# S5's Toeplitz rows and outputs: four groups one after the other in one row of PSUM, or side by side in four column tiles of TensorE

## The chip, the core and the metric

The kernel runs on one core of a Trainium2 chip. The core has TensorE (PE: matmuls, with weight loads shown apart as PEld), VectorE (DVE), ScalarE (ACT), GpSimd (POOL) and SyncE (SP), which issues most DMAs. Each engine works through its own queue in order and waits on semaphores for the others. The metric is the device time of one execution in microseconds.

## What is computed

One block of a model with two streams of 256 tokens and width 2048: modulation from two conditioning vectors, a projection `w_in`, three mixers beside each other (S5, a gated delta net, an mLSTM), a projection `w_out`, and a gated FFN. Everything is fp32. The change lies in S5, which has 32 groups of 16 channels and 64 complex states in each of two directions:

```python
def s5_run(inputs, state0, par):
    (u,) = inputs
    ab_re, ab_im, bb_re, bb_im, c_re, c_im = par
    bu_re = jnp.einsum('gph,btgh->btgp', bb_re, u)
    bu_im = jnp.einsum('gph,btgh->btgp', bb_im, u)
    ...
    ar, ai, sr, si = lax.associative_scan(complex_affine_combine, (a_re, a_im, bu_re, bu_im), axis=1)
    ...
    y = jnp.einsum('ghp,btgp->btgh', c_re, s_re) - jnp.einsum('ghp,btgp->btgh', c_im, s_im)
    return y, (s_re[:, -1], s_im[:, -1])
```

The two directions are added, `d * u` is added, and the sum goes through gelu and a gated linear unit.

## The kernel before

The kernel writes its work as generators that run beside each other. `feed` is the stream of the large matmuls (tiles `wf`, split into `wh` and `wl`, multiplied into banks `s`); each `yield` of S5 pulls so many microseconds of that stream between S5's own steps. `side` is a second stream, the modulation vectors: tiles `vw` are loaded (three buffers) and accumulated into `vacc` on VectorE, one step for one load. The program is then put in an order for each engine by a scheduler, so that rows of the order differ from the order of the text; within an engine the order is fixed when the kernel runs.

S5 works on chunks of 8 tokens. Matmuls give each chunk's contribution to the state (`s_part`), a scan on VectorE runs over the chunks (`scan`), and its states are laid out as `Sc` by two copies on VectorE and two on ScalarE. The output of a chunk is then its start state times a table `cf`, plus the chunk's own inputs `U` times a Toeplitz matrix `toe`. The 32 groups go in 8 batches of NB = 4:

- `cf_tables` builds the two parts (real and imaginary) of a batch's table, all on GpSimd: for each part 8 products of 128x128 and one sum of 128x512. Each part has two buffers, so the table of batch b+2 can begin only when `y_part(b)` has read that of batch b.
- `k_part` makes the Toeplitz rows. Matmuls `k<-cf,bz` give for each group 32 rows (16 for each direction) of 128 columns; a copy on ScalarE brings them to SBUF as `k2`; `dd`, the middle block with `d` on its diagonal, is added on VectorE. The rows are written to the scratch `kscr` in DRAM by DMAs on SP, and read back, shifted for each of 8 tokens, by four DMAs on ScalarE's queue into `toe`. (The profile calls both the matmul's bank and `k2` "k", also the bank of `dd`'s small matmuls `k<-c_re,bbre` and `k<-ncim,bbim`.)
- `y_part` makes the outputs: three matmuls for each group, `Sc` part 0, `Sc` part 1, `toe`, accumulated in the bank `y`; a copy to `yb`; after every second batch eight transposes `yT` and a copy to `yf`.

`k_part` of batches 0 and 1 runs beside the scan; then `y_part(b)` and `k_part(b+2)` alternate. After batch 7 come the gelu, the gated unit (`glu`, `sg`, `mx`), and the next stage, `gates`.

Before the change the four groups of a batch stand one after the other in the free dimension of one bank, in its partitions 0 to 31: `o_ = pk[0:32, g * P:(g + 1) * P]`, likewise for `py`. One copy of 32x512 takes a bank out. All lines are those of the functions printed here; the profile names helpers, so matmuls are L107, transposes L111, SP's DMAs L135, ScalarE's DMAs L138, products and sums L156, vacc steps L159 and L163, and ScalarE's copies L167.

Of the kernel before, what the change touches and what calls it, by code (L numbers as in the profile page):

```python
# [80 lines left out]
def body(tc, ins, out):  # L81
# [34 lines left out]
    with es:  # L116
# [885 lines left out]
        if 0 == 0:  # L1002
            z_units(m1, "stg")

        kscr = drp.tile([16, 32, 272], F32, name="kscr")
        NB = 4

        def s5(s1, s2):
# [64 lines left out]
            for g0 in range(0, 32, NB):  # L1073
                ens = []
                for part in range(2):
                    en_ = s2.tile([P, NB, 8, 16], F32, tag=f"en{part}", name="en")
                    if part == 0:
                        table(en_, pe[:, :, 0], bbre, pe[:, :, 1], bbim, g0, ALU.subtract, DVE, "ttmp")
                    else:
                        e_, t_ = (DVE, "ttmp") if g0 // NB in () else (POOL, "ttmq")  # L1080
                        table(en_, pe[:, :, 0], bbim, pe[:, :, 1], bbre, g0, ALU.add, e_, t_)
                    ens.append(en_)
                yield (1.3 if g0 else 1.3) * 1.3
                if pend is not None:
                    yield from s_part(pend, *pens)
                else:
                    bz = s1.tile([P, 2, 32, 32], F32, name="bz")
                    DVE.memset(bz, 0.0)
                    for i, b_ in enumerate((bbre, bbim)):
                        for d in range(2):  # L1090
                            r = slice(64 * d, 64 * d + 64)
                            copy(bz[r, i, :, 16 * d:16 * d + 16], b_[r].rearrange("p h g -> p g h"))
                pend, pens = g0, ens
            yield 1.3 * 1.3
            yield from s_part(pend, *pens)
# [56 lines left out]
            def k_part(b_):  # L1152
# [11 lines left out]
                   dT[:, gs].unsqueeze(2).to_broadcast([16, NB, 16]), ALU.mult)  # L1164
                yield 5.0 * 1.1
                pk = bank("k")
                for g in range(NB):
                    o_ = pk[0:32, g * P:(g + 1) * P]
                    PE.matmul(o_, bz[:, 0, g0 + g], cf[0][:, g], start=True, stop=False)
                    PE.matmul(o_, bz[:, 1, g0 + g], cf[1][:, g], start=False, stop=True)  # L1170
                k2 = s2.tile([32, NB, P], F32, tag="en0", name="k2")
                tt(dd, dd, pk0[0:16, 0:NB * 16].rearrange("p (g h) -> p g h", h=16), ALU.add)
                copy(k2.rearrange("p g c -> p (g c)"), pk[0:32])
                dma(kscr[:, gs, 0:P], k2[16:32])
                dma(kscr[:, gs, 144:272], k2[0:16])
                dma(kscr[:, gs, P:144], dd)
                toe = s2.tile([P, NB, P], F32, tag="eT", name="toe", bufs=3)
                yield 0.6 * 1.1
                for g in range(NB):
                    a = kscr[:, g0 + g, 16:144]  # L1180
                    (dma, dma_a, dma_p)[(1, 1, 1, 1)[g]](toe[:, g], bass.AP(a.tensor, a.offset, [[16, 8], list(a.ap[0]), list(a.ap[1])]))
                toes[b_] = toe

            def y_part(b_):
# [1 line left out]
                cf, toe = cfs.pop(b_), toes.pop(b_)  # L1186
                Sc = scs[0]
                py = bank("y")
                for g in range(NB):
                    o_ = py[0:32, g * P:(g + 1) * P]  # L1190
                    PE.matmul(o_, Sc[:, 0, g0 + g], cf[0][:, g], start=True, stop=False)
                    PE.matmul(o_, Sc[:, 1, g0 + g], cf[1][:, g], start=False, stop=False)
                    PE.matmul(o_, U[:, g0 + g, 32:64], toe[:, g], start=False, stop=True)
                if b_ % 2 == 0:
                    yT[0] = s1.tile([32, 8, 2 * NB, 16], F32, tag="Sctx", name="yb")
                yb = yT[0]
                copy(yb[:, :, NB * (b_ % 2):NB * (b_ % 2) + NB], py[0:32].rearrange("c (g j h) -> c j g h", j=8, h=16))
                if b_ % 2:
                    ps = bank("yT")
                    for j in range(8):  # L1200
# [926 lines left out]
```

## Time and profile before

| | us |
|---|---|
| median of 3 runs (lowest, highest) | 1821.02 (1817.79, 1821.43) |
| the profiled execution | 1827.01 |
| its span, first to last instruction | 1825.2 |
| PE busy | 1649.1 (90%) |
| DVE busy | 1111.4 (61%) |
| ACT busy | 762.3 (42%) |
| POOL busy | 443.6 (24%) |

The shares are means over stages with different limits. S5 begins at about 165 us, its scan runs from about 254 to 313, `y_part` and `k_part` alternate from 313 to 424, and the gated unit ends at about 457. A granted clock of 1.00 in a stretch is TensorE's 2.4 GHz level, 0.50 its 1.2 GHz level. An fp32 matmul of this kind is two records in the trace, so 8 records are four matmuls.

### The profile page before, as it was taken

The numbers are of one execution on the slowest core, as the hardware profiler recorded it, in microseconds if no ns is written. First come the engines' busy times: TensorE is split into PE (matmuls) and PEld (weight loads), VectorE is DVE, ScalarE is ACT, GpSimd is POOL, SyncE is SP. The second block draws the span as 40 slices with busy tenths as digits, with TensorE's granted clock in tenths as the row PEclk, the third lists the DMA queues.
The fourth block names the chain that finished last, engine by engine and source line by source line (L and its number), as shares of the span: only waits on it lengthen the run. The fifth ranks groups of instructions, "written<-read, shape, count | busy, mean of one in ns | idle before, by whom it ended". The sixth has DMA issues, their size and how long they took to land. (4 is left out here: it accounts for less than half of the span.)

```text
span 1825.2 us, 25461 instructions
## 1 busy us (share of the span) xinstructions
PE 1649.1 (90%) x9476; PEld 1336.5 (73%) x9476; DVE 1111.4 (61%) x1724; ACT 762.3 (42%) x1277; POOL 443.6 (24%) x409
## 2 busy tenths in 40 slices
PE   3986798889789998997899959999999999999998
PEld 1645687777578777776677748888888888888886
DVE  4417958666766778778544488667565454444444
ACT  3314222223354425357456475444444444443443
POOL 1014862991131343136454320000000000000001
PEclk9988998999879998999999979999999999999999
DMA  9987222667565656553222439778776666655553
GB/s 330 336 297 174 60 84 77 188 190 234 172 192 178 196 167 214 156 156 111 94 70 82 173 127 315 246 238 278 205 243 193 187 192 188 207 196 195 191 192 136
DMA packets 209202, 340.42 MB, mean 187 GB/s; under 512 B 24517, under 2 KB 68123, under 8 KB 208183
## 3 DMA queue, kind: packets, MB, share of 16 engines
q1 hardware_dynamic: 202215, 330.06, 57.3%
q0 software_dynamic: 1936, 5.60, 1.1%
q10 hardware_dynamic: 4928, 3.15, 0.6%
q8 instruction: 74, 1.21, 0.3%
q14 instruction: 49, 0.40, 0.1%
HBM read 332.11 MB, written 6.64 MB: 186 GB/s over the span
## 5 line engine op out<-in xcount | busy, mean ns | idle before, releaser
L167 ACT ACTIVATE wh<-wf 128x1024 fp32r<-128x1024 f32 (+1 forms) x404 | 420.8, 1044 | 566.5 <-PE s L107 457.7
L156 DVE TENSOR_TENSOR wl<-wf,wh 128x1024 fp32r<-128x1024 f32 (+1 forms) x350 | 430.0, 1232 | 362.9 <-ACT wh L167 359.7
L107 PE MATMUL s<-wl,h2h 128*128 128x512 f32 x704 | 276.4, 393 | 7.3 <-DVE wl L156 7.3
L107 PE MATMUL s<-wh,h2h 128*128 128x512 f32 x704 | 276.5, 394 | 6.8 <-ACT wh L167 4.1
L107 PE MATMUL s<-wh,h2l 128*128 128x512 f32 x704 | 276.3, 392 | 1.7 <-DVE h2l L156 1.7
L159 DVE SCALAR_TENSOR_TENSOR vacc<-vw,cT,vacc 128x512 f32<-128x512 f32 x240 | 204.4, 852 | 78.5 <-DMA vw<-in_ada_w_dram 75.4
L156 POOL TENSOR_TENSOR wl<-wf,wh 128x1024 fp32r<-128x1024 f32 x54 | 134.7, 2495 | 268.1 <-ACT wh L167 226.0
L156 POOL TENSOR_TENSOR rs<-ss,mhalf 128x1 f32<-128x1 f32 x6 | 4.8, 798 | 747.4 <-ACT ps L167 747.4
L107 PE MATMUL s<-hh,wh 128*128 128x512 f32 (+1 forms) x448 | 170.9, 394 | 3.3 <-ACT hh L167 3.3
L107 PE MATMUL s<-hh,wl 128*128 128x512 f32 (+1 forms) x448 | 164.1, 372 | 6.5 <-DVE wl L156 4.8
L107 PE MATMUL s<-hl,wh 128*128 128x512 f32 (+1 forms) x448 | 166.3, 372 | 0.0
L107 PEld LDWEIGHTS s<-wl,h2h 128*128 128x128 f32 x704 | 133.4, 189 | 35.7 <-DVE wl L156 8.1
L107 PEld LDWEIGHTS s<-wh,h2h 128*128 128x128 f32 x704 | 133.3, 189 | 35.5 <-ACT wh L167 5.2
L107 PEld LDWEIGHTS s<-wh,h2l 128*128 128x128 f32 x704 | 133.4, 190 | 29.8 <-DVE h2l L156 2.1
L107 PE MATMUL s<-wh,ah 128*128 128x512 f32 x352 | 136.8, 390 | 0.0
L107 PE MATMUL s<-wh,al 128*128 128x512 f32 x352 | 136.6, 389 | 0.0
L107 PE MATMUL s<-wl,ah 128*128 128x512 f32 x352 | 136.6, 389 | 0.0
L107 PEld LDWEIGHTS s<-hh,wh 128*128 128x128 f32 x448 | 89.0, 200 | 22.0 <-ACT hh L167 7.0
L107 PEld LDWEIGHTS s<-hh,wl 128*128 128x128 f32 x448 | 87.6, 197 | 22.2 <-DVE wl L156 6.1
L107 PE MATMUL s<-wh,mix 128*128 128x512 f32 x256 | 102.6, 428 | 0.1
L107 PEld LDWEIGHTS s<-hl,wh 128*128 128x128 f32 x448 | 88.8, 198 | 15.8 <-issue 3.6
L107 PE MATMUL s<-wl,hh 128*128 128x256 f32 (+1 forms) x256 | 89.6, 352 | 9.8 <-DVE wl L156 9.3
(576 smaller groups left out, 2806.6 us busy)
## 6 DMA issues: line engine op xcount, KB each, us to landing
vw<-in_ada_w_dram SPq DMA_DIRECT2D x256, 256.0 KB
wf<-in_ffn_w_gate_dram SPq DMA_DIRECT2D x96, 512.0 KB
wf<-in_w_in_dram SPq DMA_DIRECT2D x92, 512.0 KB
wf<-in_ffn_w_up_dram SPq DMA_DIRECT2D x88, 512.0 KB
wf<-in_ffn_w_down_dram SPq DMA_DIRECT2D x88, 512.0 KB
wf<-in_ada_w_dram SPq DMA_DIRECT2D x32, 1024.0 KB
wf<-in_w_out_dram SPq DMA_DIRECT2D x32, 512.0 KB
x<-in_x_dram SPq DMA_DIRECT2D x4, 1024.0 KB
```

Of the source, the lines that this page charges most:

```text
L107: return cls.queue(nc.tensor.matmul(*a, **k))
L156: return (eng or DVE).tensor_tensor(out=o, in0=a, in1=b, op=op)
L159: return (eng or DVE).scalar_tensor_tensor(out=o, in0=a, scalar=s, in1=b, op0=op0, op1=op1)
L167: return ACT.activation(out=o, in_=a, func=f, **kw)
```

## The change

For `k` and `y` the matmul of group g writes partitions 32g to 32g+31 of the bank, columns 0 to 127, and the loops run over the parts outside and over the groups inside. The `k` bank is copied out as one 128x128; `bz` holds the two directions' columns the other way round, so that one DMA for each group writes both halves of its rows; `kscr` has the group as its first dimension. The `y` bank is copied out in four pieces of 32x128, on VectorE and ScalarE in turn.

```diff
-        kscr = drp.tile([16, 32, 272], F32, name="kscr")
+        kscr = drp.tile([32, 16, 272], F32, name="kscr")
...
-                            copy(bz[r, i, :, 16 * d:16 * d + 16], b_[r].rearrange("p h g -> p g h"))
+                            copy(bz[r, i, :, 16 - 16 * d:32 - 16 * d], b_[r].rearrange("p h g -> p g h"))
...
                 pk = bank("k")
+                for i in range(2):
+                    for g in range(NB):
+                        PE.matmul(pk[32 * g:32 * g + 32, 0:P], bz[:, i, g0 + g], cf[i][:, g], start=(i == 0), stop=(i == 1))
+                k2 = s2.tile([P, P], F32, tag="en0", name="k2")
+                tt(dd, dd, pk0[0:16, 0:NB * 16].rearrange("p (g h) -> p g h", h=16), ALU.add)
+                copy(k2, pk[:, 0:P])
                 for g in range(NB):
-                    o_ = pk[0:32, g * P:(g + 1) * P]
-                    PE.matmul(o_, bz[:, 0, g0 + g], cf[0][:, g], start=True, stop=False)
-                    PE.matmul(o_, bz[:, 1, g0 + g], cf[1][:, g], start=False, stop=True)
-                k2 = s2.tile([32, NB, P], F32, tag="en0", name="k2")
-                tt(dd, dd, pk0[0:16, 0:NB * 16].rearrange("p (g h) -> p g h", h=16), ALU.add)
-                copy(k2.rearrange("p g c -> p (g c)"), pk[0:32])
-                dma(kscr[:, gs, 0:P], k2[16:32])
-                dma(kscr[:, gs, 144:272], k2[0:16])
-                dma(kscr[:, gs, P:144], dd)
+                    a = kscr[g0 + g, :, 0:P]
+                    dma(bass.AP(a.tensor, a.offset, [[144, 2]] + [list(v) for v in a.ap]), k2[32 * g:32 * g + 32])
+                dma(kscr[gs, :, P:144].rearrange("g h x -> h g x"), dd)
...
-                    a = kscr[:, g0 + g, 16:144]
+                    a = kscr[g0 + g, :, 16:144]
...
                 py = bank("y")
-                for g in range(NB):
-                    o_ = py[0:32, g * P:(g + 1) * P]
-                    PE.matmul(o_, Sc[:, 0, g0 + g], cf[0][:, g], start=True, stop=False)
-                    PE.matmul(o_, Sc[:, 1, g0 + g], cf[1][:, g], start=False, stop=False)
-                    PE.matmul(o_, U[:, g0 + g, 32:64], toe[:, g], start=False, stop=True)
+                for i in range(3):
+                    for g in range(NB):
+                        w, m = (U[:, g0 + g, 32:64], toe[:, g]) if i == 2 else (Sc[:, i, g0 + g], cf[i][:, g])
+                        PE.matmul(py[32 * g:32 * g + 32, 0:P], w, m, start=(i == 0), stop=(i == 2))
...
-                copy(yb[:, :, NB * (b_ % 2):NB * (b_ % 2) + NB], py[0:32].rearrange("c (g j h) -> c j g h", j=8, h=16))
+                for g in range(NB):
+                    (DVE.tensor_copy, copy)[g % 2](yb[:, :, NB * (b_ % 2) + g],
+                                                   py[32 * g:32 * g + 32, 0:P].rearrange("c (j h) -> c j h", h=16))
```

The scheduler's order changes with it. On TensorE, at `y_part(0)` right after the scan, before (here `cf_1825` and `cf_1836` are parts 0 and 1 of batch 0's table, `y_2541` the bank):

```order
L107 MATMUL y_2541<-cf_1825,Sc_2535 32x128 [waits DVE_49,Activation_49]
L107 MATMUL k0_2578<-c_re_335,bbre_391 16x16
L107 MATMUL k0_2578<-ncim_400,bbim_392 16x16
L107 MATMUL k0_2578<-c_re_335,bbre_391 16x16
L107 MATMUL y_2541<-cf_1836,Sc_2535 32x128 [waits DVE_49,Activation_49]
L107 MATMUL y_2541<-toe_1915,U_1128 32x128 [waits DMAHW2_49]
L107 MATMUL y_2541<-cf_1825,Sc_2535 32x128
L107 MATMUL y_2541<-cf_1836,Sc_2535 32x128
L107 MATMUL y_2541<-toe_1915,U_1128 32x128 [waits DMAHW4_49]
```

and after, from the same place to the second k pack of batch 2 (`k_2684`; `y_2712` is `y_part(1)`):

```order
L107 MATMUL y_2545<-cf_1825,Sc_2539 32x128 [waits DVE_49,Activation_49]
L107 MATMUL y_2545<-cf_1825,Sc_2539 32x128 x3
...
L107 MATMUL y_2545<-cf_1836,Sc_2539 32x128 [waits DVE_49,Activation_49]
L107 MATMUL y_2545<-cf_1836,Sc_2539 32x128 x3
L107 MATMUL y_2545<-toe_1917,U_1128 32x128 [waits DMAHW2_49]
...
L107 MATMUL k_2684<-cf_2563,bz_1208 32x128 [waits Pool_49]
L107 MATMUL k_2684<-cf_2563,bz_1208 32x128 x3
L107 MATMUL y_2712<-cf_1943,Sc_2539 32x128 [waits DVE_49]
...
L111 MATMUL yT_2729<-ident_112,yb_2558 128x32 [waits PE_49,Activation_49]
...
L107 MATMUL k_2684<-cf_2574,bz_1208 32x128 [waits Pool_49]
```

All reads of part 0 now stand ahead of the first read of part 1, and the transposes yT, which wait for the copies of batches 0 and 1, stand ahead of the second k pack. Before, 18 matmuls of s stood between `vm` and batch 2's first k; now the 51 that come next stand behind the second pack.

On VectorE, at the same place, before:

```order
L1147 COPY Sc<-Sq 64x1024 [waits DVE_49]
L1147 COPY Sc<-Sq 64x1024
L156 TENSOR_TENSOR wl<-wf,wh 128x1024 [waits DMAHW2_49,Activation_49]
L156 TENSOR_TENSOR dd<-dd,k_2578 16x64 [waits PE_49]
L156 TENSOR_TENSOR mod_1099<-vm,cols 128x4 [waits PE_49]
L163 TENSOR_SCALAR vacc<-vw,cT 128x512 [waits DMAHW4_49]
L156 TENSOR_TENSOR dd<-ident,dT 16x64 [waits DMAHW5_49,DVE_49]
L159 SCALAR_TENSOR_TENSOR vacc<-vw,cT,vacc 128x512 [waits DVE_49] x2
```

and after, where the copies of batch 0 stand at the head and those of batch 1 behind six vacc steps:

```order
L1197 COPY yb<-y 32x8x16 [waits DVE_49,PE_49,Activation_49]
L156 TENSOR_TENSOR dd<-dd,k_2585 16x64 [waits PE_49]
L1197 COPY yb<-y 32x8x16 [waits Activation_49]
L156 TENSOR_TENSOR mod_1099<-vm,cols 128x4 [waits PE_49]
L163 TENSOR_SCALAR vacc<-vw,cT 128x512 [waits DMAHW4_49]
...
L1197 COPY yb<-y 32x8x16 [waits PE_49]
L159 SCALAR_TENSOR_TENSOR vacc<-vw,cT,vacc 128x512 [waits DMAHW6_49,DVE_49]
L1197 COPY yb<-y 32x8x16 [waits Activation_49]
```

In the middle of the vacc steps VectorE now waits for TensorE's y and for ScalarE's copy of the group before; ScalarE's own yb copies wait for VectorE in turn.

On SP, at batch 7's writes, before:

```order
L135 DMA kscr<-k_3522 16x4x128 [waits DMAHW3_49,Activation_49]
L135 DMA kscr<-k_3522 16x4x128
L135 DMA vw<-in_ada_w_dram 128x512 [waits DMAHW7_49,DVE_49]
L135 DMA vw<-in_ada_w_dram 128x512 [waits DMAHW6_49,DMAHW0_49,DVE_49]
L135 DMA wf<-in_w_in_dram 128x2x512 [waits DMAHW3_49,DVE_49]
```

and after:

```order
L135 DMA kscr<-k_3554 2x16x128 [waits Activation_49]
L135 DMA kscr<-k_3554 2x16x128
L135 DMA vw<-in_ada_w_dram 128x512 [waits DMAHW6_49,DMAHW0_49,DVE_49]
L135 DMA kscr<-k_3554 2x16x128
L135 DMA vw<-in_ada_w_dram 128x512 [waits DMAHW2_49,DVE_49]
L135 DMA vw<-in_ada_w_dram 128x512 [waits DMAHW4_49,DMAHW3_49,DVE_49]
L135 DMA kscr<-k_3554 2x16x128 [waits DMAHW5_49]
```

The four writes of a batch are divided by vw loads that wait for VectorE.

## Rows read from the trace of the kernel before

**Rows 1.** Busy us (instructions) by stretch: PE, PEld, DVE, ACT, POOL; clock, DMA share, GB/s

```profile
305.20:313.00 7.80, 0.24 (x3) 0.04 (x1) 7.25 (x32) 1.96 (x2) 0.00 (x0) 0.80 0.00 0
313.00:319.00 6.00, 4.94 (x28) 4.05 (x29) 1.23 (x2) 2.88 (x2) 0.00 (x0) 0.50 0.11 25
319.00:408.40 89.40, 77.29 (x615) 66.30 (x613) 56.50 (x72) 19.52 (x37) 84.64 (x108) 0.96 0.64 186
408.40:424.00 15.60, 14.30 (x85) 11.82 (x86) 6.14 (x9) 3.28 (x5) 0.00 (x1) 0.89 0.62 195
...
440.00:455.00 15.00, 11.67 (x55) 9.04 (x56) 8.70 (x13) 4.98 (x7) 3.20 (x2) 1.00 0.96 305
455.00:520.00 65.00, 46.81 (x229) 37.62 (x228) 46.68 (x71) 26.89 (x44) 14.07 (x11) 0.85 0.65 205
...
1150.00:1800.00 650.00, 650.00 (x2926) 539.37 (x2925) 347.25 (x336) 273.94 (x287) 0.00 (x0) 1.00 0.67 210
```

**Rows 2.** GpSimd in time order: start, us, line, operation, count [idle before <-releaser]

```profile
319.01 4.43 POOL L156 TENSOR_TENSOR cf<-pf,c_re 128x128 f32<-128x128 f32 x8 [18.87 <-PE y L107]
...
335.35 4.23 POOL L156 TENSOR_TENSOR ttmp<-pf,c_im 128x128 f32<-128x128 f32 x4
...
341.00 1.80 POOL L156 TENSOR_TENSOR ttmp<-pf,c_im 128x128 f32<-128x128 f32 x4
...
366.01 5.10 POOL L156 TENSOR_TENSOR cf<-pf,c_re 128x128 f32<-128x128 f32 x8 [3.57 <-PE y L107]
...
406.81 1.59 POOL L156 TENSOR_TENSOR cf<-cf,ttmp 128x512 f32<-128x512 f32 x1
```

**Rows 3.** TensorE's matmuls in time order, two records for one matmul

```profile
313.03 0.64 PE L107 MATMUL y<-cf,Sc 128*32 128x128 f32 x2 [7.59 <-DVE Sc L1147]
...
314.88 0.63 PE L107 MATMUL y<-cf,Sc 128*32 128x128 f32 x2 [1.03 <-ACT Sc L167]
...
318.29 1.06 PE L107 MATMUL y<-cf,Sc 128*32 128x128 f32 x4
...
365.55 0.60 PE L107 MATMUL y<-cf,Sc 128*32 128x128 f32 x4
...
378.01 1.72 PE L107 MATMUL k<-cf,bz 128*32 128x128 f32 x14 [0.42 <-POOL cf L156]
```

**Rows 4.** The ada matmuls in four column tiles, and their weight loads (PEld)

```profile
21.29 1.93 PE L107 MATMUL ada<-wf,csz 128*32 128x512 f32 x8 [0.78 <-DMA wf<-in_ada_w_dram]
...
51.20 1.07 PE L107 MATMUL ada<-wf,csz 128*32 128x512 f32 x8
52.20 2.00 PE L111 MATMUL xt<-ident,x 128*128 128x128 f32 x16
...
51.20 0.16 PEld L107 LDWEIGHTS ada<-wf,csz 128*32 128x32 f32 x8 [0.17 <-issue]
```

**Rows 5.** Small copies out of PSUM, grouped by line: count, busy us, mean ns

```profile
L167 ACT ACTIVATE vn<-st 128x128 f32<-128x128 f32 x24 | 6.5, 272 | 2.2 <-PE st L107 2.0
...
L1309 DVE COPY bec<-beT 128x48 f32<-128x48 f32 x1 | 0.2, 202 | 0.0
```

**Rows 6.** ScalarE and its DMA queue (ACTq) in time order, batch 7

```profile
412.73 0.59 ACT L167 ACTIVATE k<-k 32x512 f32<-32x512 f32 x1 [5.52 <-PE k L107]
...
419.02 2.45 ACTq L138 DMA_DIRECT2D toe<-kscr  x4
...
423.90 0.59 ACT L167 ACTIVATE yb<-y 32x512 f32<-32x512 f32 x1 [0.32 <-PE y L107]
```

**Rows 7.** SP's DMA issues in time order, batch 7's two writes

```profile
414.91 0.85 SPq L135 DMA_DIRECT2D kscr<-k  x2
```

**Rows 8.** VectorE's vacc steps in time order, first and last of nine

```profile
321.25 0.76 DVE L163 TENSOR_SCALAR vacc<-vw,cT 128x512 f32<-128x512 f32 x1
...
328.41 3.48 DVE L159 SCALAR_TENSOR_TENSOR vacc<-vw,cT,vacc 128x512 f32<-128x512 f32 x3 [0.53 <-DMA vw<-in_ada_w_dram]
```

**Rows 9.** Who waited for whom, 424 to 600 us: total, times, longest

```profile
ACT wh L167 <- DMA wf<-in_w_in_dram: 22.0, 7, 6.7
```

## Prediction

> **What bounds the kernel now.** I read the stretches first. From 1150 to 1800 us TensorE is busy in every microsecond [rows 1], so nothing there can hide a late start: whatever S5 gains or loses is likely to reach the end. The change lies in S5, whose last part runs from 313 to about 455 us. In its largest piece, 319.0 to 408.4, GpSimd is busy 84.64 of 89.40 us, TensorE 77.29, VectorE 56.50 and ScalarE 19.52 [rows 1]: GpSimd, which builds the cf tables (16 small products and two sums of 128x512 for a batch), is what fills the time. Its own rows say when it starts and stops [rows 2]. It starts at 319.01 after 18.87 us of waiting for "PE y", that is, until y_part(0) has read the cf tables of batch 0 and their two buffers are free; it waits once more, 3.57 us, again for "PE y", before 366.01; the last sum starts at 406.81. Then TensorE's rows [rows 3]: y_part(0) begins at 313.03, when Sc is there, and its last group at 318.29.
>
> So the question is not how much TensorE time the packing saves, but how much earlier cf is free and how soon the results leave after the last table.
>
> **The change part by part, by TensorE time.** A 128-column fp32 matmul is two records. Unpacked and at the high clock, 14 records took 1.72 us [rows 3], 0.12 each, so four groups (8 records) are 0.98 us. What four column tiles cost shows in the ada matmuls at the head of the kernel, which are laid out this way, in fp32, with 512 columns: 8 records, the next work 1.00 us later, and their eight weight loads within 0.16 us [rows 4]. A quarter of the columns gives 0.25 us as an estimate. Bounds for a pack: 0.25 and 0.98 us; I take 0.25, since the ada rows are the same form. There are 8 x 2 packs of k and 8 x 3 of y, so 40 x 0.73 = 29 us less TensorE work, 0 at the other bound. Of this nearly all turns into waiting for GpSimd, since GpSimd has 4.76 us of slack in the 89.40 and TensorE 12.11.
>
> A page speaks against the packing. The Trainium skill, "TensorE: Matmul & The Clock Gate", Part 3 on row/col tiling, says that weight loads overlap running matmuls only where the row groups differ; column tiles share them, and a pack would then pay its loads, too. With the row's 0.16 us a pack would be 0.41 instead of 0.25, some 6 us over 40 packs, off the path; no row here separates the two, and if the loads weigh more than that, it is the third rival.
>
> **The start of GpSimd's chain.** Before, y goes group by group, and cf part 0 is read last by group 3, at 318.29; GpSimd starts 0.72 later [rows 2, 3]. After, the four matmuls on cf part 0 stand first (the first pair of order listings). They start at 313.03 as before, waiting for Sc. The clock is at its low level there: granted 0.50 from 313 to 319, after 7.8 us in which TensorE was busy 0.24 [rows 1]; a pack of 512 columns at that level took 1.93 us [rows 4], a quarter is 0.48. With 0.3 us to the release (0.72 less the 0.42 of two records, from 0.64 and 1.06 for two and four [rows 3]) GpSimd starts at 313.8: 5.2 us earlier. Part 1 is free at about 315.7, as its matmul waits for ScalarE's Sc until 314.88 [rows 3]; GpSimd is then at the end of its first four products (a free one 0.45, from 1.80 for four [rows 2]). Without overlap of the packs it would be 4 x 0.42 = 1.7, so 315.0: 4.0 us earlier.
>
> **The second wait.** The 3.57 us before 366.01 stand behind group 3 of y_part(3), which TensorE had after seven matmuls of k(4) and a run of s; it was done at 365.55 to 366.15 [rows 2, 3]. Now both cf parts of a batch are read in eight matmuls right behind the first k pack. I count 2.6 us won: 3.6, less 1.0 for a new wait where k(6) stands in the same row of packs as y(5). Bounds 0 and 3.6.
>
> **GpSimd's own pace.** Four products took 1.80 us free and 4.23 beside VectorE's work [rows 2]. VectorE gets 16 small copies more (0.2 to 0.3 each by the nearest rows, VectorE's copy of 128x48 and ScalarE's of 128x128, both out of PSUM [rows 5]), 3 to 5 us in all, but no further vacc or wl. Bounds -2 and +3 us; I take +1.0.
>
> **The tail.** Before, after the last sum (406.81) come k(7), its copy on ScalarE from 412.73, the two kscr writes at 414.91, four toe reads from 419.02 and the yb copy at 423.90 [rows 2, 6, 7]: 15 us of latency. After, k(7) has one pack left when the sum is done, so the copy starts some 3 us sooner, at a shorter 0.27 for 0.59. Against it stand four writes of one group each, with three vw loads between them in SP's order, each waiting for a vacc step of VectorE. Such a step is 1.2 us: from 321.25 to 331.89 VectorE made nine and a small one [rows 8]. That takes back 0 to 4 us. I take -2.0 in sum, bounds -4 and +1.
>
> **The new chain of copies.** The four yb copies alternate VectorE, ScalarE, VectorE, ScalarE, and each waits for the one before (second pair of listings). Behind ScalarE's copies stand the next wh and the toe reads; behind VectorE's the wl; and TensorE's yT waits for the last of the eight. For batch 1 I can follow it: vacc starts at about 317.6 instead of 321.25 (y(0) ends some 3.6 us sooner), seven steps at 1.2 us and the copies end at about 327.5, and only then come yT, the second k pack of batch 2 and 51 matmuls of s, some 6 us, to about 335. GpSimd's table for batch 3 is due at about the same time, so this costs nothing as long as the vw loads come at the old pace, and microsecond for microsecond beyond it. I take +1.5 for all batches; bounds 0 and +14 (below).
>
> **What follows S5.** From 440 to 455 the DMA engines are 0.96 busy, and ScalarE waits 22.0 us for wf in 424 to 600 [rows 1, 9]. Part of a gain can end there: I take +1.0, bounds 0 and +7.
>
> **The sum.** -5.2 - 2.6 + 1.0 - 2.0 + 1.5 + 1.0 = -6.3 us. The profiled execution took 1827.0 us (span 1825.2 and 1.8 around it), 6.0 above the median of 1821.0; 1827.0 - 6.3 = 1820.7 there, and 1821.0 - 6.3 = 1814.7 for the median.
>
> **The rivals.**
> *The gain is absorbed (same).* The chain starts early, but the stretch behind S5 is set by DMA. For: 0.96 in 440 to 455. Against: from 455 to 520 it is 0.65, TensorE busy 46.81 of 65 [rows 1], so the rest can move up. With +6 instead of +1 behind S5: 1820.
> *The chain of copies decides (slower).* Between the first and the last VectorE copy of the eight batches stand about a dozen other steps in VectorE's order (dd, mod, vacc, wl); at 1.2 us each that is 14 us in which the y bank, yT and ScalarE's wh are held. It decides when vw loads come later than one in 1.2 us, as the cover at batch 3 is then gone. All on the path: -6.3 - 1.5 + 14 = +6.2, so 1827. For: VectorE sits in the middle of loads here; against: VectorE is free for 33 of 89 us [rows 1]. Beside it stands a rule of the Trainium skill, "TensorEngine Tiling (Array Packing)", PSUM Bottleneck: after such a speedup the copies out of PSUM may become the bottleneck, to be shared by ScalarE and VectorE and joined over tiles of a bank. Here a joined copy is divided in four; no row of before shows such a handoff.
> *The packs do not overlap (faster, less).* For: weight loads come once in 0.03 us here, once in 0.125 in the ada rows [rows 4]; against: those eight fit into 0.16 us. Then 4.0 for 5.2, and one us less in the tail: -4.1, so 1816.9.
>
> **How the numbers follow.** Chances: forecast 0.57, packs without overlap 0.06, absorbed 0.20, copies decide 0.17. Within 0.2% is 3.6 us, about what a measurement of this kernel can tell from no change; faster 0.63, same 0.20, slower 0.17. The forecast's own range is 1806 (second wait gone whole, tail -4, contention -2, nothing given back) to 1819. To hold 8 in 10 it must reach through the absorbed case and to the edge of the slower one: 1806 to 1825.
>
> **What would show it.** After: GpSimd's first cf product at about 313.8; no idle of 3 us before a cf for "PE y"; k and y packs as eight records in 0.25 to 0.3 us at the high clock; TensorE waiting longer for "POOL cf"; the last cf sum near 400 instead of 407; glu some 6 to 8 us sooner. Wrong if GpSimd starts past 315, if ScalarE waits for VectorE's yb by more than 10 us in sum, if TensorE waits for yT, or if the gap to before at 455 is gone by 520.

## The result: 1.0% faster, more than twice the forecast

| | before | after |
|---|---|---|
| median of 5 runs, us (lowest, highest) | 1821.43 (1817.79, 1822.51) | 1807.77 (1794.99, 1809.92) |
| ratio to before (95% interval) | | 0.9899 (0.987, 0.9927) |
| the profiled execution, its span | 1827.0, 1825.2 | 1807.8, 1806.0 |

The forecast was 1814.7, a gain of 6.3 us; by the ratio 18 us were gained, by the medians 13.7. A second measurement of the changed kernel gave 1805.53 and a ratio of 0.9911 (0.9894, 0.9927), some 16 us. The direction held, and the first median lies in the range (1806 to 1825), the second 0.5 us below it; the size didn't hold.

**S5's chain.** GpSimd's rows after, in time order (start, us, ..., idle before and its releaser), answer to [rows 2]:

```profile
311.06 3.69 POOL L156 TENSOR_TENSOR cf<-pf,c_re 128x128 f32<-128x128 f32 x8 [16.50 <-PE y L107]
...
384.65 4.71 POOL L156 TENSOR_TENSOR cf<-pf,c_re 128x128 f32<-128x128 f32 x8 [0.73 <-PE y L107]
...
395.32 1.26 POOL L156 TENSOR_TENSOR cf<-cf,ttmp 128x512 f32<-128x512 f32 x1
```

TensorE's rows after, in time order, answer to [rows 3]:

```profile
310.30 0.66 PE L107 MATMUL y<-cf,Sc 128*32 128x128 f32 x8 [8.20 <-DVE Sc L1147]
...
312.19 0.65 PE L107 MATMUL y<-cf,Sc 128*32 128x128 f32 x8 [0.79 <-ACT Sc L167]
...
345.50 0.42 PE L107 MATMUL k<-cf,bz 128*32 128x128 f32 x8
345.74 0.62 PE L107 MATMUL y<-cf,Sc 128*32 128x128 f32 x16
```

GpSimd starts 0.76 us behind y_part(0) (311.06 - 310.30) where it was 5.98, and a pack costs TensorE 0.24 us (345.50 to 345.74). Both are as forecast.

**Where the time went.** I cut both executions at the same four events: y_part(0), the end of the last cf sum, the first glu matmul, the last mo matmul of the mLSTM. Busy us (instructions) of PE, PEld, DVE, ACT, POOL, then TensorE's clock, DMA share and GB/s, for each stretch; before:

```profile
313.03:408.40 95.37, 82.23 (x641) 70.34 (x641) 57.72 (x73) 22.37 (x39) 84.64 (x108) 0.93 0.61 176
408.40:432.95 24.55, 23.25 (x128) 18.95 (x129) 11.92 (x16) 8.03 (x10) 0.00 (x1) 0.93 0.69 220
432.95:579.10 146.15, 124.39 (x622) 100.27 (x620) 100.53 (x172) 64.17 (x123) 32.68 (x21) 0.88 0.59 184
579.10:1825.20 1246.10, 1174.52 (x6756) 971.91 (x6755) 750.38 (x969) 574.30 (x958) 207.49 (x140) 0.98 0.58 184
```

and after:

```profile
310.30:396.58 86.28, 63.72 (x637) 54.77 (x638) 53.53 (x81) 18.76 (x43) 83.62 (x108) 0.81 0.63 180
396.58:425.76 29.18, 23.69 (x118) 16.76 (x118) 19.40 (x26) 9.39 (x14) 2.56 (x1) 0.82 0.82 256
425.76:556.32 130.56, 116.59 (x626) 95.66 (x626) 93.39 (x170) 63.21 (x123) 28.25 (x20) 0.96 0.64 198
556.32:1806.00 1249.68, 1183.77 (x6749) 979.32 (x6748) 749.08 (x969) 573.56 (x957) 211.10 (x140) 0.97 0.58 184
```

Each kernel was profiled a second time. Lengths of the stretches in us, first and second profile:

| stretch | before | after | mean difference |
|---|---|---|---|
| start to y_part(0) | 313.0, 312.1 | 310.3, 312.9 | -1.0 |
| to the end of the last cf sum | 95.4, 94.0 | 86.3, 87.5 | -7.8 |
| to the first glu (the tail) | 24.6, 22.9 | 29.2, 31.7 | +6.7 |
| to the last mo | 146.2, 147.2 | 130.6, 132.9 | -14.9 |
| to the end | 1246.1, 1247.8 | 1249.7, 1245.0 | +0.4 |

So S5 as a whole, from y_part(0) to the first glu, is shorter by only 1.1 us: what GpSimd wins, the tail loses. The gain stands in the next stretch, the gated unit, the gates and the mLSTM, where no instruction was changed. The difference is there in both pairs of profiles (15.6 and 14.3 us), so it is no accident of one execution.

**What differs there.** Busy us by stretch again, from the first glu to the gates' first transpose (gcT) and from there to the last mo; before:

```profile
432.95:473.53 40.58, 28.56 (x146) 23.37 (x144) 24.81 (x28) 18.83 (x24) 9.65 (x4) 0.92 0.65 206
473.53:579.10 105.57, 95.83 (x476) 76.90 (x476) 75.72 (x145) 45.34 (x99) 23.02 (x17) 0.87 0.56 176
```

and after:

```profile
425.76:466.55 40.79, 33.63 (x176) 29.19 (x176) 22.93 (x30) 19.92 (x26) 7.12 (x3) 0.92 0.67 208
466.55:556.32 89.77, 82.96 (x452) 66.47 (x451) 70.45 (x141) 43.29 (x98) 21.14 (x17) 0.98 0.63 194
```

In the same 41 us TensorE does 30 matmul records more (176 for 146), at the cost of its idle time; behind gcT it has 24 fewer (452 for 476). These are records of the stream, most of them of 256 columns, which follow each other in 0.12 us at the high clock, the others of 512 columns in 0.23: some 3 us. Another 3 of the 16 us are idle time (9.7 to 6.8), and the rest goes with the clock (0.87 to 0.98). In the second profiles more of the gain is idle time and less is clock: from the first glu to the last mo TensorE's idle time falls from 21.4 to 11.0 us there (first profiles: 21.8 to 14.0), and the clock rises from 0.88 to 0.90 (0.88 to 0.96). The first mo matmuls of the first profiles, before and after (TensorE in time order):

```profile
517.94 1.23 PE L107 MATMUL mo<-va,Dm 128*128 128x129 f32 x4 [5.42 <-DVE Dm L156]
```

```profile
504.10 0.68 PE L107 MATMUL mo<-va,Dm 128*128 128x129 f32 x4 [1.97 <-DVE Dm L156]
```

Before, TensorE waits 5.42 us for VectorE's Dm and then runs four records in 1.23 us; after, it waits 1.97 and takes 0.68. Over all mo matmuls the granted clock was 0.86 before (row in the next section) and 1.00 after:

```profile
504.10:556.32 52.22, 52.22 (x299) 42.11 (x299) 36.99 (x87) 29.43 (x72) 10.71 (x9) 1.00 0.53 160
```

The order there was made anew by the scheduler, as it was for the whole program.

### The profile page after: what moved, and what is told of

The parts are those of the page before. It is cut to its first block, busy times and chain, and to the rows that moved or that the text cites. A ratio compares the mean times of both kernels' runs of the same rounds, so it can differ in the third digit from the quotient of the medians.

```text
span 1806.0 us, 25520 instructions
## 1 busy us (share of the span) xinstructions
PE 1630.2 (90%) x9476; PEld 1319.8 (73%) x9476; DVE 1105.9 (61%) x1740; ACT 758.6 (42%) x1285; POOL 440.6 (24%) x409
## 5 line engine op out<-in xcount | busy, mean ns | idle before, releaser
L107 PEld LDWEIGHTS s<-hh,wh 128*128 128x128 f32 x448 | 90.0, 202 | 21.1 <-ACT hh L167 6.5
```

What stands on the lines that cost most here:

```text
L107: return cls.queue(nc.tensor.matmul(*a, **k))
```

## The experiments

Each kernel ran on one chip beside the kernel before; a ratio is to that.

**Is it chance, and is it the packing or the order of the reads?** The two kernels once more:

> The kernel before, profiled once more. The comparison of the two first profiles has 19.2 us between them: 2.7 arise ahead of y_part(0), 4.5 between it and the first glu matmul, 15.6 between that and the last mo matmul of the mLSTM (146.2 us before, 130.6 after), and 3.6 are lost again later. Theory A (the order of the program sets the stretches behind S5): this profile has 145 to 148 us again from the first glu matmul to the last mo, with TensorE idle some 5 us ahead of the first mo and the clock at its low level during the mo matmuls. Rival B (these stretches differ from execution to execution, through the clock): it lies elsewhere, somewhere between 130 and 146, while the stretch from y_part(0) to the last cf sum (95.4) repeats within 1 us.

> The changed kernel, profiled once more. Theory A: 130 to 132 us from the first glu matmul to the last mo, again without the low clock there. Rival B: between 130 and 146. Both: GpSimd's first cf product of batch 2 starts 0.7 to 0.9 us after y_part(0) (5.98 before), the last cf sum ends 86 to 87 us after it (95.4 before). Ratio to the kernel before 0.987 to 0.993.

Measured: 1823.84 us, ratio 1.0007 (0.9989, 1.0026), and 1805.53, 0.9911 (0.9894, 0.9927); the stretches are in the table above. Glu to last mo is 147.2 and 132.9 (0.9 above its range), so theory A holds against B. But what it says of the clock fails: in the second profile of the changed kernel the mo matmuls start after a wait of 1.31 us and still run at a mean clock of 0.88. So the length of the wait ahead of mo (1.97 us in the first profile, with a clock of 1.00) does not decide it.

Loops alone, in the old layout (k in the same way, flags fitted so that a bank is opened once):

```diff
-                for g in range(NB):
-                    o_ = py[0:32, g * P:(g + 1) * P]
...
+                for i in range(3):
+                    for g in range(NB):
+                        w, m = (U[:, g0 + g, 32:64], toe[:, g]) if i == 2 else (Sc[:, i, g0 + g], cf[i][:, g])
+                        PE.matmul(py[0:32, g * P:(g + 1) * P], w, m, start=(i + g == 0), stop=(i + g == NB + 1))
```

> The kernel before with the loops over parts outside and over groups inside, in the old layout (one row of four groups, one copy, two kscr writes). Theory C (the early release of cf, that is the order of the reads, gives the gain in GpSimd's chain, the packing little): four unpacked matmuls on part 0 at the low clock take 4 x 0.42 = 1.7 us, so the first cf product starts about 2.0 us after y_part(0), and the last cf sum ends some 88 us after it; the time is 5 to 8 us below before, 0.996. Rival D (the packing gives it, as TensorE's time in this stretch is what counts): the last cf sum ends later than 91 us after y_part(0), and the time is within 3 us of before.

Layout alone:

```diff
-                for i in range(3):
-                    for g in range(NB):
+                for g in range(NB):
+                    for i in range(3):
```

> The changed kernel with the loops over groups outside again, so that the four column tiles stay but a group's matmuls follow each other. Theory C: cf part 0 is then read last by group 3, at the end of y_part; the first cf product starts some 3.5 to 5 us after y_part(0) and the last cf sum ends 90 us or more after it; most of the gain up to there is gone, the time lies 8 us or less below before. Rival D: the layout alone keeps the gain, the last cf sum ends at 86 to 88 us.

Measured: the loops alone 1818.96, 0.9984 (0.997, 0.9998); the layout alone 1813.58, 0.995 (0.9933, 0.9967). GpSimd started 2.00 and 3.89 us behind y_part(0), as theory C has it. The last cf sum ended 94.0 us behind it with the loops alone, where C had 88 and rival D more than 91 and a time within 3 us of before, which it is; with the layout alone it ended 91.0 us behind it, as C has it. In single profiles the early start alone is lost again along the chain, and packs with late reads keep half of what both together win there.

**Fill the idle time, pack one of the two, join the writes.**

```diff
-                yield 5.0 * 1.1
+                yield 6.0 * 1.1
```

> The changed kernel with one number changed: each k_part pulls 6.0 for 5.0 units of the stream between its tables and its k matmuls, which puts 43 stream records more between y_part(0) and the first glu matmul. Two theories of where the time went. Theory E (TensorE's sum decides from y_part(0) to the end: the packing took some 24 us of k and y out of it, 9 to 10 us of which stand as idle time beside GpSimd's chain in S5; whatever stream fills that idle time is gone from the later stretches): 43 records of 0.23 us are 10 us; the idle time from y_part(0) to the last cf sum falls from 23 to about 13, the cf chain is as long as before (86 to 88), and the time falls by 4 to 10 us to about 1798 to 1802. Rival F (the stream in S5 hangs on vw and wf loads and the splits, so it can't come sooner): the cf chain or the tail grow by as much, the time is 1803 to 1812.

> The changed kernel with y_part of before (group by group, one row, one copy); only k is packed. Theory E: k is 16 of the 40 packs, so TensorE's work falls by 0.4 of 24 us, 10 us; the first cf product starts 6.0 us after y_part(0) as before; time 1811 to 1816. Theory C (the early release of cf alone brings the gain): as y still frees cf late, the gain is under 3 us, 1818 to 1822.

> The kernel before with y_part of the change (parts outside, four column tiles, four copies); k, its copy and its writes as before. Theory E: y is 24 of the 40 packs, 14 us of TensorE's 24; first cf product 0.8 us after y_part(0); time 1806 to 1811. Theory C: nearly the whole gain, 1804 to 1808, and the cf chain ends 86 to 88 us after y_part(0).

```diff
-                            copy(bz[r, i, :, 16 - 16 * d:32 - 16 * d], b_[r].rearrange("p h g -> p g h"))
+                            copy(bz[r, i, :, 1 - d:32:2], b_[r].rearrange("p h g -> p g h"))
...
-                for g in range(NB):
-                    a = kscr[g0 + g, :, 0:P]
-                    dma(bass.AP(a.tensor, a.offset, [[144, 2]] + [list(v) for v in a.ap]), k2[32 * g:32 * g + 32])
+                a = kscr[gs, :, 0:P]
+                dma(bass.AP(a.tensor, a.offset, [[272, 16 * NB], [144, 2], [1, P]]), k2)
```

> The changed kernel with the two directions' columns of bz interleaved, so that one DMA writes all rows of a batch to kscr in place of four. The stretch from the last cf sum to the first glu matmul was 22.9 to 24.6 us before and 29.2 to 31.6 after. Theory G (the four writes, divided by vw loads in SP's order, hold the toe reads of batch 7 and so y, yT and glu): it falls to 24 to 26 us, and the time by 3 to 6 us to 1800 to 1803. Rival H (the yb copies in VectorE's order hold it): it stays at 28 to 31 us, and the time at 1804 to 1808.

Measured: filled 1822.84, 0.9992 (0.9969, 1.0014); k only 1821.36, 0.9982 (0.9968, 0.9997); y only 1822.63, 0.9999 (0.9974, 1.0024); one write 1819.5, 0.998 (0.9962, 0.9998). Theory E's times are missed by all three of its kernels; k only lies where theory C has it, but y only, which frees cf as early as the whole change (0.77 us), wins nothing, against both: its cf chain takes 94.0 us and its tail 33.9. Filled, the cf chain took 100.2 us for 86 to 88 while TensorE still stood idle 22.8 us of it: theory E fails here, the stream can't simply be put into S5, and the time is above rival F's range, too. One write left the tail at 32.2 us: theory G fails, and the time is not where H had it. And a kernel that differs from the changed one by that write and the order of bz's columns alone is some 13 us slower, with the same cf chain (85.5); its first mo waits 6.44 us, and glu to last mo takes 138.2. From the first glu to the end it takes 1391.3 us, for 1380.2 and 1377.9 in the changed kernel: a small edit of S5 moved the time behind S5 by 11 to 13 us, nearly as much as the change itself did (1392.3 and 1395.0 before).

**The copies in the tail.**

```diff
-                    (DVE.tensor_copy, copy)[g % 2](yb[:, :, NB * (b_ % 2) + g],
-                                                   py[32 * g:32 * g + 32, 0:P].rearrange("c (j h) -> c j h", h=16))
+                    copy(yb[:, :, NB * (b_ % 2) + g],
+                         py[32 * g:32 * g + 32, 0:P].rearrange("c (j h) -> c j h", h=16))
```

> The changed kernel with all four yb copies on ScalarE. Last cf sum to first glu was 22.9 to 24.6 us before and 29.2 to 31.6 after; one write of kscr for four left it at 32.2. Theory H (the yb copies that alternate between VectorE and ScalarE, and stand behind vacc and wl steps, make the tail longer): it falls to 21 to 25 us; ScalarE waits for no yb of VectorE. Rival Q (the tail follows the vw loads and the toe reads, not the copies): it stays at 28 us or more. The time depends on where the order behind S5 puts the rest: 1800 to 1820.

Measured: 1810.42, 0.993 (0.9911, 0.9949); the tail 21.1 us for 29.2 to 31.7. The changed kernel's ScalarE in the tail (ACTq is its DMA queue):

```profile
402.31 0.27 ACT L167 ACTIVATE yb<-y 32x128 f32<-32x128 f32 x1
403.95 2.33 ACTq L138 DMA_DIRECT2D toe<-kscr  x3
406.32 0.27 ACT L167 ACTIVATE yb<-y 32x128 f32<-32x128 f32 x1 [3.74 <-DMA kscr<-k]
409.49 0.58 ACTq L138 DMA_DIRECT2D toe<-kscr  x1
...
417.08 0.27 ACT L167 ACTIVATE yb<-y 32x128 f32<-32x128 f32 x1 [2.74 <-DVE yb L1197]
418.05 0.27 ACT L167 ACTIVATE yb<-y 32x128 f32<-32x128 f32 x1 [0.71 <-DVE yb L1197]
```

its VectorE at the last batch:

```profile
415.63 1.22 DVE L156 TENSOR_TENSOR wl<-wf,wh 128x1024 fp32r<-128x1024 f32 x1
416.77 0.27 DVE L1197 COPY yb<-y 32x128 f32<-32x128 f32 x1
416.97 0.73 DVE L159 SCALAR_TENSOR_TENSOR vacc<-vw,cT,vacc 128x512 f32<-128x512 f32 x1
417.73 0.28 DVE L1197 COPY yb<-y 32x128 f32<-32x128 f32 x1
```

and ScalarE with all four copies there:

```profile
404.11 1.11 ACT L167 ACTIVATE yb<-y 32x128 f32<-32x128 f32 x4 [2.88 <-PE y L107]
...
416.35 1.11 ACT L167 ACTIVATE yb<-y 32x128 f32<-32x128 f32 x4 [0.18 <-PE y L107]
```

A copy is 0.27 us on either engine, so the four cost 1.11 in a row on ScalarE. In turns they wait for what stands between them in VectorE's order, a wl here and a vacc there, and ScalarE's queue, the toe reads among it, waits with them. The first three rows of who waited for whom, 310 to 426 us after (total, times, longest), have it second:

```profile
POOL wl L156 <- ACT wh L167: 26.4, 1, 26.4
ACT yb L167 <- DVE yb L1197: 24.9, 11, 9.5
DVE vacc L159 <- DMA vw<-in_ada_w_dram: 19.6, 20, 4.1
```

With the copies on ScalarE alone no such row is left, and the tail is as short as theory H has it: S5 from y_part(0) to the first glu is then 108.7 us, some 9.7 less than before. Not all of that is waiting for copies, as the edit changed TensorE's order, too. The last transposes, in the changed kernel and with all copies on ScalarE:

```profile
421.62 0.68 PE L111 MATMUL yT<-ident,yb 32*128 32x32 f32 x8
```

```profile
417.51 0.68 PE L111 MATMUL yT<-ident,yb 32*128 32x32 f32 x8 [0.54 <-ACT yb L167]
```

In the changed kernel they start 3.3 us behind the last copy (418.05 + 0.27), with matmuls of the stream ahead of them; with the copies on ScalarE they start when the last copy is done. But glu to last mo is 142.4 us there, 11 more than in the changed kernel, and the time is no better.

**What decides the stretch behind S5?** One number behind S5, in both kernels; the order up to gcT stays what it was in each:

```diff
-            feed.lo, side.rate = 2, 0.3
+            feed.lo, side.rate = 2, 0.1
```

> The kernel before with one number changed behind S5: the side stream's rate there is 0.1 for 0.3, so the 14 vacc steps that stand on VectorE between gcT and the mLSTM's first mo are put later. The order up to gcT is that of before. Theory O (the 15 us that the change gained between the first glu matmul and the last mo come from where the scheduler puts such steps, not from the packing itself; the wait of TensorE ahead of the first mo, 4.4 to 5.4 us before and 1.3 to 2.0 after, then decides whether the clock falls during the mo matmuls): gcT to first mo falls from 45 to 36 us or so, the wait ahead of mo to under 2, and glu to last mo from 147 to 130 to 136; the time falls by up to 12 us to 1811 to 1817 though nothing is packed, less what comes back when the steps are made up. Rival P (TensorE's smaller load by packing is needed for it): glu to last mo stays above 142, time 1820 to 1826.

> The changed kernel with the same one number (side rate 0.1 for 0.3 behind S5). Theory O: the wait ahead of mo is small already, so little is left to win there; glu to last mo 126 to 133 us, time within 5 us of the changed kernel, 1801 to 1811. Rival P: the gain of the packing and that of the number add, glu to last mo falls below 122, time below 1797.

Measured: before with it 1832.85, 1.0054 (1.0034, 1.0074); the changed kernel with it 1822.87, 1.0 (0.9981, 1.0019). The number acts at the place that was meant, but the times lie outside theory O's ranges and rival P's in both kernels. The first mo of the kernel before with that number, without a wait, and its mo stretch:

```profile
506.98 0.61 PE L107 MATMUL mo<-va,Dm 128*128 128x129 f32 x4
```

```profile
506.98:566.24 59.26, 58.27 (x341) 47.59 (x339) 42.60 (x94) 31.19 (x73) 12.83 (x9) 1.00 0.53 168
```

against, in the kernel before,

```profile
517.94:579.10 61.16, 61.16 (x316) 49.74 (x316) 41.54 (x88) 30.73 (x72) 14.26 (x10) 0.86 0.45 139
```

The clock stays at 1.00, 25 records more fit into 1.9 us less, and glu to last mo is 140.8. But from there to the end it takes 1264.7 us for 1246.1 to 1247.8, more than was won. Nine vacc steps more stand in that part; that they are the reason is not shown. The changed kernel does the same: 129.5 us from glu to last mo, as theory O has it, and 1261.7 for 1245.0 to 1249.7 behind it.

The other number of that line, every wl on GpSimd (`1, 0.3`), and the side rate at 0.4 (`2, 0.4`), in pairs:

> The kernel before with another number behind S5: every wl there is made on GpSimd in place of every second one. The order up to gcT is that of before. Theory O: VectorE loses some 6 steps of 1.2 us ahead of mo, GpSimd's take 2.5 each; the stretch from gcT to the first mo changes by several us, and glu to last mo comes out anywhere between 132 and 150, with the clock low during the mo matmuls only where the wait ahead of mo is over 4 us. Rival P: as before within 3 us, 144 to 150.

> The changed kernel with every wl behind S5 on GpSimd, beside the kernel before with the same number (1827.1 us). It moves three or four wl steps near the gated unit off VectorE. Theory O2 (two parts: the packing itself is worth 8 to 12 us, as the pair with the side rate at 0.1 showed, 10.0; the rest of the 16 us of the first comparison is the place where the order behind S5 happens to fall): the pair's difference is 8 to 12 us, 1815 to 1819. Rival P2 (the whole 16 us belong to the packing): 15 us or more, 1812 or less.

> The kernel before with the side rate behind S5 at 0.4 for 0.3; the order is that of the kernel before until within the mo matmuls. Both theories: glu to last mo 144 to 149 us, with the clock at its low level for some 20 us of the mo matmuls, as before. Its time is the base for the pair: 1815 to 1830.

> The changed kernel with the side rate behind S5 at 0.4 for 0.3; the order is that of the changed kernel until within the mo matmuls. Theory O2: time 1803 to 1818, 8 to 12 us below the kernel before with the same number. Rival P2: 15 us or more below it.

Measured, kernel before, then the changed kernel:

| behind S5 | before, us and ratio | after, us and ratio | pair |
|---|---|---|---|
| as it is | 1823.84, 1.0007 | 1805.53, 0.9911 | -18 |
| side rate 0.1 | 1832.85, 1.0054 | 1822.87, 1.0 (0.9981, 1.0019) | -10 |
| every wl on GpSimd | 1827.06, 1.0017 (0.9998, 1.0036) | 1809.98, 0.994 (0.9917, 0.9963) | -14 |
| side rate 0.4 | 1817.32, 0.9976 (0.9961, 0.9991) | 1800.97, 0.9894 (0.986, 0.9928) | -16 |

(The third pair was run on two chips, so its difference is taken from the ratios.) The changed kernel wins in each. The number in the third row moved fewer steps than I had expected, three or four wl near the gated unit, and glu to last mo was as before there, 146.8 (137.8 in the changed kernel with that number, some 6 more than without). Theory O2 (8 to 12 us) fits the second pair alone, from which it was made; the third lies between it and P2, the fourth with P2. But the pairs share their order up to gcT, the part in which the 30 records are moved, so they don't tell packing and order apart. That was the last test's part, in the kernel before:

```diff
                 dma(mixd[n], mx)
-                yield 0.65
+                yield 1.5
```

> The kernel before with one number changed in the gated unit behind S5: the second yield of its loop is 1.5 for 0.65. Nothing is packed, and the order up to the gated unit is that of before; the program's order then has 144 stream records between the first glu and gcT for 112 (142 in the changed kernel) and 225 for 243 between gcT and the last mo (218). Theory O3 (the 13 to 15 us that the change gains behind S5 are this placing: stream records put where TensorE waits for the gated unit and the gates, 12 us before and 5 to 7 after): glu to last mo falls from 146 to 130 to 138 us, with less low clock, and the time by 6 to 14 us to 1808 to 1816. Rival R (the records can be placed there only because the packing freed TensorE or left other loads): glu to gcT gets longer by as much, 46 us or more for 40, glu to last mo stays over 142, time 1818 or more.

Measured: 1820.58, 0.9981 (0.9962, 0.9999). By stretch, first glu to gcT to last mo:

```profile
421.69:467.69 46.00, 36.44 (x186) 32.00 (x185) 27.75 (x41) 20.29 (x26) 7.84 (x3) 0.85 0.78 246
467.69:572.00 104.31, 94.02 (x451) 74.07 (x450) 68.13 (x141) 44.22 (x99) 20.55 (x17) 0.87 0.56 171
```

The records were moved (186 for 146, 451 for 476), but gcT came 5 to 6 us later for it, and behind it the stretch was only 1 to 3 us shorter. Theory O3 falls in this form: where the records stand isn't enough. Rival R's three numbers are all met; its reason, that the packing made room for the records, was not tested apart from that.

**Both edits of the tail, and the two best numbers together.**

> The changed kernel with both edits of the tail: one write of kscr for a batch, and all yb copies on ScalarE. Theory H: last cf sum to first glu 20 to 22 us, as with the copies on ScalarE alone (21.1), since the writes were not what held the tail. Rival G: below 19 us. The time follows the order behind S5: 1800 to 1815.

> The changed kernel with all yb copies on ScalarE (1810.4 us alone) and the side rate of 0.4 behind S5 (1801.0 alone). If the two gains add, as theory H with the order left as it is has it, 1792 to 1799; if the order behind S5 decides (O), as with the copies alone, 1803 to 1812.

Measured: 1816.99, 0.9962 (0.9941, 0.9982), tail 25.4 us; and 1809.78, 0.9897 (0.9851, 0.9943), tail 23.1, glu to last mo 143.1. The first lies above theory H's tail (20 to 22) and rival G's (below 19), the second where theory O has it: the gains do not add. The side rate of 0.4 in the changed kernel, 1800.97, has the lowest median, but its ratio can't be told from that of the changed kernel.

## Why the forecast had the direction and not the size

Steps that were right:

- *The start of GpSimd's chain*: -5.2 us forecast, -5.2 measured (5.98 to 0.76).
- *What a pack costs*: 0.25 forecast, 0.24 at the high clock. By the rule of the Trainium skill ("TensorE: Matmul & The Clock Gate", Part 3) that loads overlap only where row groups differ it would have been 0.41 here by the prediction's estimate; the trace disagrees. TensorE's busy time on the tiles k and y from y_part(0) to the first glu, dd's small matmuls among them, fell from 47.3 to 23.2 us.
- *A change in S5 reaches the end*: the last 1246 us are the same in both.

Steps that failed, the first ahead of the sum, the others in its order:

- *Nearly all of the TensorE work that is saved turns into waiting for GpSimd.* In S5 it did turn into waiting: from y_part(0) to the first glu TensorE's idle time rose from 14 (95.37 - 82.23 + 24.55 - 23.25) to 28 us (86.28 - 63.72 + 29.18 - 23.69). But TensorE waited less for GpSimd's cf than before, and it waited 8 us at the first yT for the yb copies, which the prediction had named as a sign of being wrong. Who TensorE waited for in that stretch (total, times, longest), before:

```profile
PE k L107 <- POOL cf L156: 9.9, 7, 2.8
```

  and after:

```profile
PE yT L111 <- ACT yb L167: 8.0, 1, 8.0
...
PE k L107 <- POOL cf L156: 2.4, 3, 0.9
```

  In the second profiles it is 10.5 before, 7.9 and 0.9 after. The wait at yT itself cost S5 nothing that shows: with all copies on ScalarE it is 1.3 us, the waits for cf are 10.0 again, and the cf chain is as long (87.6). And over the whole program the saving did not turn into waiting, as the end of this section shows. So the prediction's sum had no term for TensorE's smaller work, and that is where the gain of the first comparison stands.
- *The second wait* (-2.6) and *GpSimd's own pace* (+1.0) were both wrong, and the errors nearly cancelled. The second profile of before had a wait of 1.36 us, not 3.57, and the changed kernel's two profiles 0.73 and 2.94 + 1.27; on average nothing was won. GpSimd's busy time, in turn, fell by 2.5 us (84.6 and 85.5 to 83.6 and 81.4).
- *The tail* (-2.0, bounds -4 to +1) and *the new chain of copies* (+1.5, bounds 0 to +14) were sized -0.5 together and came to +6.7. The mechanism was named, as the slower rival, and its place was wrong: I followed the copies through batch 1, where GpSimd's tables cover them, and not through the last two batches, where nothing does. With the copies on one engine, and the order that came with it, the tail is 8 to 11 us shorter. ScalarE's 24.9 us of waiting for VectorE's yb, most of it ahead of the tail, is the other sign that the prediction had named for this (more than 10 us in sum).
- *What follows S5* (+1.0, bounds 0 to +7) measured -14.9. This term made the miss in size. I asked how much of a gain would be absorbed, and so excluded a gain from that stretch without a reason, although the scheduler orders all of it anew when S5 changes.

So the forecast was closer than its working deserved, which is luck: S5 gave 1.1 us for the 7.3 of its terms, and the stretch behind it gained 15 where 1 was to be lost.

How much of those 15 belongs to the packing can be told only in part. TensorE's busy time over the whole program (PE) was, before and after, in the first profiles:

```profile
PE 1649.1 (90%) x9476; PEld 1336.5 (73%) x9476; DVE 1111.4 (61%) x1724; ACT 762.3 (42%) x1277; POOL 443.6 (24%) x409
```

```profile
PE 1630.2 (90%) x9476; PEld 1319.8 (73%) x9476; DVE 1105.9 (61%) x1740; ACT 758.6 (42%) x1285; POOL 440.6 (24%) x409
```

The second profiles have 1648.9 and 1628.9. TensorE's idle time, the rest of the span, is 176.1 and 175.0 us before, 175.8 and 181.0 after. So the gain of the first comparison is the smaller busy time of TensorE, 19 to 20 us, and little of it came back as idle time. In all ten kernels here with k and y packed TensorE is busy for 1621.2 to 1633.9 us, in the six with neither for 1645.1 to 1651.4: this part goes with the packing in every order. What differs within a group is mostly the idle time, 173.9 to 193.4 us with the packing and 167.7 to 182.5 without.

The times follow: over the ten the ratio runs from 0.9894 to 1.0, its mean is 0.9945; over the six it runs from 0.9976 to 1.0054, mean 1.0003. They are no random sample. A difference of 11 us between the groups, with 14 to 19 us between the ends of each, is the best that I can say of packing as such; the changed kernel also won in four pairs, by 10 to 18 us. Against reading the 15 us behind S5 as the packing's alone: the loops alone, with nothing packed, have 137.3 us from glu to last mo (and 1251.5 behind it), and with the copies on ScalarE, with everything packed, it is 142.4. Why the idle time behind the first glu fell in the changed kernel stays open. What was ruled out as the sole cause: chance, the vacc steps ahead of mo, and the number of stream records ahead of gcT.

## What to carry to other kernels

Where a scheduler orders the whole program, the change of one stage is also a new draw for the stages behind it: compare by stretches between the same events, profile both kernels twice, and give the range of such a draw (here 10 us either way) beside the sum of the forecast. Add up the busy and the idle time of the engine that fills the later stages, too: work taken off it can come out there, though a chain on another engine bounds the stage that was changed. Four column tiles brought four small fp32 matmuls here from 0.98 us (estimated from [rows 3]) to 0.24, but look first at who takes the four pieces out: copies dealt out in turns to two engines wait for whatever stands between them on either, and in the last batch nothing covers that. An early release of a shared buffer won nothing along GpSimd's chain here without a cheaper pass over the buffer, and the cheaper pass alone half of what the two won together.

## What was unexpected in the hardware's behaviour

- More idle time on TensorE in S5 went with a lower clock: from y_part(0) to the last cf sum the granted clock was 0.93 and 0.94 before and 0.81 and 0.78 after (rows by stretch above for the first profiles). TensorE's busy time there still fell, from 82 to 64 us.
- VectorE's last `mx` took 2.81 us for 0.65 in both profiles of before. GpSimd had begun a wl just ahead of it; VectorE, then GpSimd, in the first profile:

```profile
450.62 0.65 DVE L156 TENSOR_TENSOR mx<-yf,sg 128x256 f32<-128x256 f32 x1
...
454.33 2.81 DVE L156 TENSOR_TENSOR mx<-yf,sg 128x256 f32<-128x256 f32 x1
```

```profile
454.16 2.50 POOL L156 TENSOR_TENSOR wl<-wf,wh 128x1024 fp32r<-128x1024 f32 x1 [4.91 <-ACT wh L167]
```

  After, no `mx` starts while a wl of GpSimd runs, in either profile, and all four are 0.62 to 0.68 us long: at most 2.2 of the 15 us. That the wl is the cause is not shown, as nothing else was held fixed.
- The eight weight loads of a k pack lie within 0.18 us while the pack itself takes 0.24, so loads into column tiles run beside the matmuls of the same pack; TensorE's loads (PEld) in the changed kernel:

```profile
393.25 0.18 PEld L107 LDWEIGHTS k<-cf,bz 128*32 128x32 f32 x8
```
